# A decoder layer on one core: a first chunk's product one place later, a sum in another buffer, a split ahead of copies, and unit runs that end in half depths

## The chip, the cores and the metric

The kernel runs on one core of a Trainium2 chip. The metric is device time in microseconds (us) of one launch. The engines are called TensorE (PE; PEld is its weight load), VectorE (DVE), ScalarE (ACT), GpSimd (POOL) and SyncE (SP, which issues the transfers).

## The reference, cut to what matters

```
mod = silu(c) @ w_ada + b_ada                       # six rows: shift, scale, gate for two sub-layers
h = rms_norm(x, g_pre_mix) * (1 + sc_m) + sh_m      # x is 1024 tokens x 1024
proj = h @ w_in                                     # 256 pooling channels, then q, k, v: 12 heads of 64
q, k = partial_rope(q), partial_rope(k)
o_g = dilated_window_attention(q, k, v)             # three groups of 4 heads: dilation 1, 4, 16
attn = sum_g softmax_over_g(lse_g) * o_g
x = x + gt_m * rms_norm(concat(pool(u), attn) @ w_out, g_post_mix)
h = rms_norm(x, g_pre_ffn) * (1 + sc_f) + sh_f
gate, val = split(h @ w_up)                         # 2 x 2816 columns
y = (gelu(causal_conv3(gate)) * val) @ w_down
x = x + gt_f * rms_norm(y, g_post_ffn)
```

All is float32. The kernel multiplies float32 by splitting each factor in a high part and the rest (a copy on ScalarE that rounds, and a subtraction on VectorE, called the lower) and adding three products: high by high, high by low, low by high.

## The kernel before, in words

The attention stage handles six units, each one dilation group and one pair of heads, in the order (2,0), (1,0), (0,0), (2,1), (1,1), (0,1); a unit's number in the code is `ui`, from 0. `project(un, prev)` runs the unit's input product over eight token tiles `t`, each eight deep in `k` (`mm`, which calls `proj_mm`, three matmuls of 128x384, and then `Q.tick()`). So one unit has 64 ticks. The queue `Q` carries out the attention of the unit before, a piece at a time, on ticks: turning q and k (`turn_qk`, L621), scores (L680), turning the weights (L700), weighing values (L710) and turning the merged result (`turn_a`, L752). The tile's product lies in PSUM bank `t % 2`; `evac` copies q and k to SBUF on ScalarE (L265) and v on VectorE (L267, L270). Two tiles make a pair `m`, which is then rotated (`rope`). The unit's weights lie in four pieces of two `k` each (`ws[k // 2]`). The buffers for pieces number six; the next unit's pieces are asked for at ticks 2, 10, 50 and 56, so its third and fourth take the buffers of the current unit's first two (split: ScalarE L123, VectorE L170). In this stage only TensorE's order is the order of the text; the orders of the other engines are chosen when the program is compiled.

Behind it comes the channel sub-layer, in which the order of every engine but SyncE is the order of the text. Its first product, a chunk of 128 gate and 128 value columns at a time (22 chunks `c`), is computed by seven products of half size instead of eight (a Strassen-Winograd form). Four half-size sums of the activations (`sums`, on VectorE) and their splits (`parts`) are made once, in column halves `lo_t` and `hi_t`. A product `(n, c)` has twelve matmuls of 128x512. Products 1 and 2 of the first four chunks run ahead; then a list `steps` sets the order of the rest: places 0 to 3 are (5,0), (6,0), (3,0), (7,0), written out by hand, places 4 to 8 are (5,1), (6,1), (4,0), (3,1), (7,1), and place 9 is (5,2). Product 4 of chunk 0 needs the split of activation block "22", which is made only when chunk 0's others are on their way.

`prep(n, c)` makes a product's weights: for n of 5, 6, 7 and 4 a sum on GpSimd (`total`, L1158: t1, t2, t3, t4), then the high copy on ScalarE (L123); the lower (L1154) is returned and called a place or so later by `prep_up(to, low)`, which prepares up to place `to` and calls the lowers below `low`. Sums and fetched weights take their buffers in turn from `pool_r`; the pieces take theirs in turn from `ring`, of which `more0` lies in the memory of the activations that "22" is split from. The loaded weights of a chunk lie in `raw4`; t4 of chunk 0 is made in the buffer `b21`. `later_evac` puts the evictions of a product one place later (`at_step`): n of 6 frees the banks of 5 and 6, 3 and 7 and 4 their own; 4 is followed by the convolution's taps (L1189, L1191), a gelu on ScalarE and the gating product (L1196). PSUM has eight banks, taken in the order in which they came free.

Of the kernel before, what the change touches and what calls it, by code (L numbers as in the profile page):

```python
# [76 lines left out]
TURN_AT = ((5, 5, 0, 0), (6, 2, 0, 1), (6, 7, 1, 0), (7, 2, 1, 1), (8, 3, 2, 0), (8, 7, 2, 1), (9, 7, 3, 0), (10, 3, 3, 1))  # L77
# [27 lines left out]
def block_kernel(ctx: ExitStack, tc: tile.TileContext, x, pos, cols, rows, consts, w_ada_a, w_ada_b, w_in_u,  # L105
# [155 lines left out]
    def evac(un, t, b):  # L261
        m, j = divmod(t, 2)
        if m not in un.qs:
            un.qs[m] = bq.tile([P, 2, 256], F32, name="qs", tag="qs", bufs=2)
        nc.scalar.activation(un.qs[m][:, j], PS[:, b, 0:256], AF.Copy)  # L265
        if un.g == 0:
            nc.vector.tensor_copy(un.V[:, t], PS[:, b, 256:384])  # L267
            return
        vs = bq.tile([P, P], F32, name="vs", tag="vs", bufs=2)
        nc.vector.tensor_copy(vs, PS[:, b, 256:384])  # L270
        if un.g == 1:
            dst = vscr[1].rearrange("(r n i) c -> n i r c", r=4, n=2)[t // 4, 32 * (t % 4):32 * (t % 4) + 32]
        else:
            dst = vscr[2].rearrange("(r i) c -> i r c", r=16)[8 * t:8 * t + 8]
        nc.sync.dma_start(dst, vs)
# [14 lines left out]
    un = Unit(0, None)  # L290
# [308 lines left out]
    with tc.tile_pool(name="bp", bufs=1) as bp, tc.manual_schedule(engines={ET.PE}):  # L599
# [39 lines left out]
        def project(un, prev):  # L639
            def mm(t, lo=0, hi=NK):  # L640
                for k in range(lo, hi):
                    proj_mm(bank(t % 2, 384), t, un.ws, k)
                    Q.tick()

            def turned(m):
                Q.after(LAG_QK if un.ui else LAG_0, lambda: turn_qk(un, m), lambda: prev is None or prev.scored == NT)

            if un.ui == 0:
                turned(0)
                for m in (1, 2):  # L650
                    mm(m + 5, 0, 4)
                    for t in range(2 * m, 2 * m + 2):
                        evac(un, t, t)
                    rope(un, m)
                    turned(m)
            for m in range(0 if un.ui else 3, 4):
                for t in range(2 * m, 2 * m + 2):
                    mm(t, 0 if un.ui else 4)
                    evac(un, t, t % 2)
                rope(un, m)  # L660
                turned(m)
# [150 lines left out]
        for ui in range(5):  # L812
            if ui:
                un = Unit(ui, ws)
# [27 lines left out]
        un = Unit(5, ws)  # L842
# [34 lines left out]
    if True:  # L877
# [56 lines left out]
        def parts(name, cols, of=(0, 1), lo_eng=None):  # L934
            for k, h, l in A[name][of[0]:of[-1] + 1]:
                split(SRC[name][:, k:k + h.shape[1], cols], h[:, :, cols], l[:, :, cols], lo_eng=lo_eng)
# [10 lines left out]
        def sums(cols, which):  # L947
            m11, m12, m21, m22, m1 = (x[:, :, cols] for x in (a11, a12, a21, a22, SRC["s1"]))
            for i in which:
                o, a, b, op = ((m1, m22, m21, ALU.subtract), (m11, m1, m11, ALU.add), (m12, m11, m12, ALU.subtract),  # L950
                               (m21, m11, m22, ALU.subtract))[i]
                nc.vector.tensor_tensor(o, a, b, op)
# [25 lines left out]
        if True:  # L978
            def slot(key):
                if key in TURNS:  # L980
                    x_turn(*TURNS[key])
                    h_split(*TURNS[key])
# [11 lines left out]
            for c in range(AHEAD + 1):  # L994
                if c == 0:
                    up_load(2)
                    up_load(3)
                if c == 2:
                    raws = [rp.tile([P, 2, 512], F32, name="raws", tag="raw") for _ in range(2)]
                    raws = [t[:, i] for t in raws for i in range(2)]  # L1000
                    for i in range(4):
                        nc.sync.dma_start(raws[i], w_up[0, :, i])
                    b11, b21, b12, b22 = raws
                    t2r = cp.tile([P, 512], F32, name="t2r", tag="macc")
                    p0 = r2.tile([P, 4, 512], F32R, name="p0", tag="r2b")
                    ring += [(p0[:, i], p0[:, i + 1]) for i in (0, 2)]
                    TR["t4", 0] = b21
                for n in range(8):
                    slot((8 + c, n))
                    if (8 + c, n) == FIRST_T:  # L1010
                        start_sum("t1", b11, b11, b12)
                        start_sum("t2", t2r, b11, b22)
                        start_piece("t1", b11)
                        start_piece("t2", t2r)
                    if (8 + c, n) == TURN_AT[-2][:2]:
                        sums(lo_t, range(4))
                        parts("s1", lo_t)
                        parts("s2", lo_t)
                    if (8 + c, n) == LAST_X:
                        stats((), (NT - 1,))  # L1020
                        s1 = r2.tile([P, 2] + half[1:], F32R, name="s1", tag="r2c")
                        A["s1"] = [(0, s1[:, 0], s1[:, 1])]
                        SRC["s1"] = r2.tile(half, F32, name="s1t", tag="r2a")
                        pairs_of("s2")
                    wh, wl = (x[:, n * P:(n + 1) * P] for x in wu[c])
                    ah, al = side("11" if n < 4 else "12", n % 4)
                    o = bank(SLOTS[c][n // 4])
                    nc.tensor.matmul(o, wh, ah, start=n % 4 == 0, stop=False)
                    nc.tensor.matmul(o, wh, al, start=False, stop=False)
                    nc.tensor.matmul(o, wl, ah, start=False, stop=n % 4 == 3)  # L1030
# [25 lines left out]
            def first(c):  # L1056
                if c < NC_FF:
                    first_copy(c)
                    first_add(c)
# [73 lines left out]
            A["22"] = [(0, *(r2.tile(half, F32R, name="b22", tag=t) for t in ("r2a", "r2b")))]  # L1133
            s1g = cp.tile([P, 512], F32, name="s1g", tag="cst")
            gm = r1.tile(half, F32, name="gm", tag="rb1")
            pool_r = [b22, b11, b12, gm[:, 2], gm[:, 3], b21]

    gscr = tc.dram_tile([NC_FF // 2, 7, P, 512], F32, name="gscr")
    gtf_d = tc.dram_tile([1, D], F32, name="gtf_d")
    if True:  # L1140
# [70 lines left out]
        steps, done, START_AT = [], AHEAD, {}  # L1211
        for c in range(NC_FF):
            START_AT[c] = len(steps)
            one = []
            if c not in SKIP and done < NC_FF - 1:
                done += 1
                one = [done]
            ahead = [(n, k) for n in (2, 1) for k in one]
            old = [(4, c - 1)] * (c > 0)
            if c in SKIP or not ahead:  # L1220
                steps += [(5, c), (6, c)] + old + [(3, c), (7, c)]
            else:
                steps += [(5, c)] + old + [(6, c)] + ahead + [(3, c), (7, c)]
        steps.append((4, NC_FF - 1))
# [30 lines left out]
        def at_step(i, f, rank=0):  # L1255
            tasks.append((i, rank, len(tasks), f))
            tasks.sort(key=lambda t: t[:3])
# [21 lines left out]
            for kb in range(8):  # L1279
                EXTRA.setdefault(i - 18 + 2 * kb, []).append(lambda hf=hf, kb=kb: gate_acc(hf, kb))  # L1280
        for c in range(1, NC_FF - 1):
            EXTRA.setdefault(START_AT[c] + 5, []).append(lambda c=c: at_step(now[0], lambda: first(c + 1)))

        DOWN = (1, 2, 6, 5, 3, 7, 4)
        KD = NC_FF // 2
# [32 lines left out]
        def prep_up(to, low):  # L1318
            while ready[0] < min(to, len(steps)):
                lows.append(prep(*steps[ready[0]]))  # L1320
                ready[0] += 1
            while lows and ready[0] - len(lows) < min(low, len(steps)):
                lows.pop(0)()
# [4 lines left out]
        at["p"] = 0  # L1328
        prep_up(6, 6)
        evac(3, 0)  # L1330
        parts("22", all_t)
        evac(7, 0)
        for i, (n, c) in enumerate(steps):
            if i < 4:
                continue
            now[0] = i
            for f in EXTRA.get(i, ()):
                f()
            to = i + 1 + min(LEAD, 2 + (i - 4) // 3)
            prep_up(to, to - LAG_LO)  # L1340
            left = len(steps) - i
            if left <= 5:
                if not R1:
                    R = r1.tile([P, 16, 512], F32, name="R1", tag="ra")
                    R1 += [R[:, j] for j in range(KD)]
                    extend(pool_r, "r", [raw4[0][:, j] for j in range(4)] + [R[:, j] for j in range(KD, 16)])
                for j in {5: (0, 1), 4: (2,), 3: (3,), 1: (4,)}.get(left, ()):
                    prep_down(j)
            run_tasks(i)
            while not idle:  # L1350
                run_tasks(10**6, 1)
            product(n, c)
            later_evac(n, c)
            if (n, c) == (5, NC_FF - 1):
                more = r2.tile([P, 8, 512], F32R, name="tail", tag="r2c")
                extend(ring, "p", [(more[:, 2 * j], more[:, 2 * j + 1]) for j in range(4)])
# [147 lines left out]
```

## Time and profile before

| | |
|---|---|
| median of three runs | 1061.61 us (1061.49 to 1061.78) |
| the profiled execution, its own time | 1063.7 us |
| its span, first to last instruction | 1061.8 us |
| TensorE busy | 1033.1 us, 97% of the span |
| VectorE busy | 857.9 us, 81% |
| ScalarE busy | 486.8 us, 46% |
| GpSimd busy | 217.8 us, 21% |
| mean granted clock of TensorE | 0.996 |

The busy share is an average over stages. A matmul's end is modelled, so idle time of TensorE is better read from starts than from ends. A granted clock of 1.00 is 2.4 GHz, 0.50 would be 1.2 GHz, and a number between is a stretch that had both.

### The profile page before, as it was taken

Reading aid. Unit: us, or ns where it says so; the run is one execution under the profiler, and the core shown is the slowest. Engines: PE = TensorE matmul, PEld = TensorE weight load, DVE = VectorE, ACT = ScalarE, POOL = GpSimd, SP = SyncE. Lnnn points to the kernel's source line nnn. Section 1 sums busy time; section 2 is a strip of 40 time slices with the busy share of each in tenths; the row PEclk is TensorE's granted clock in tenths of the full one; section 3 lists DMA queues with packets and bytes.
Section 4 is the critical chain, followed back from the end, with each engine's and each line's share of the span. In section 5 each row is a group of like instructions: output and inputs, shape, how many; then the busy total and the mean of one; then the engine's idle time right before and its main releaser. Section 6 shows DMA issues by size and latency. Waiting matters only on the chain.

```text
span 1061.8 us, 15438 instructions
## 1 busy us (share of the span) xinstructions
PE 1033.1 (97%) x5174; PEld 875.2 (82%) x5174; DVE 857.9 (81%) x1839; ACT 486.8 (46%) x964; POOL 217.8 (21%) x132
## 2 busy tenths in 40 slices
PE   5999999999999999999999999999999999999997
PEld 4988989889888787878888888888888888888885
DVE  7974467876457768999999888999998898756998
ACT  6764343433354469643343333333333265544642
POOL 0000000000000000154433333244333415103560
PEclk9999999999999999999999999999999999999999
DMA  9552346352131173324335334444453879466563
GB/s 365 214 170 75 111 115 215 83 182 72 54 96 46 37 257 128 111 90 159 127 131 169 138 116 144 158 149 159 169 174 114 308 240 375 159 197 219 183 213 119
DMA packets 85148, 168.34 MB, mean 159 GB/s; under 512 B 9158, under 2 KB 25926, under 8 KB 81356
## 3 DMA queue, kind: packets, MB, share of 16 engines
q1 hardware_dynamic: 85068, 167.35, 46.8%
q8 instruction: 41, 0.67, 0.3%
q14 instruction: 39, 0.32, 0.1%
HBM read 134.47 MB, written 32.84 MB: 158 GB/s over the span
## 4 chain that ended last, share of the span: by engine, by line
PE 88%; DVE 5%; ACT 3%; DMA 2%; issue 2%; POOL 0%; SPq 0%; DVEq 0%; ACTq 0%; POOLq 0%
PE PS L1084 36%; PE PS L1384 20%; PE PS L221 6%; PE PS L223 5%; PE PS L222 5%; PE PS L710 3%; PE PS L680 2%; PE PS L700 1%; DVE acc L343 1%; PE PS L595 1%; PE PS L597 1%; PE PS L596 1%; DMA wa<-in_w_ada_a_dram 1%; PE PS L621 1%; PE PS L776 1%
## 5 line engine op out<-in xcount | busy, mean ns | idle before, releaser
L1158 POOL TENSOR_TENSOR raws<-rw 128x512 f32<-128x512 f32 x30 | 47.9, 1598 | 503.8 <-DVE raws L962 446.4
L221 PE MATMUL PS<-wh,hh 128*128 128x384 f32 x336 | 125.4, 373 | 1.3 <-DVE vs L270 1.2
L223 PE MATMUL PS<-wh,hl 128*128 128x384 f32 x336 | 113.8, 339 | 0.0
L222 PE MATMUL PS<-wl,hh 128*128 128x384 f32 x336 | 113.5, 338 | 0.0
L1084 PE MATMUL PS<-a,more 128*128 128x512 f32 x408 | 95.4, 389 | 0.0
L1384 PE MATMUL PS<-tail 128*128 128x512 f32 x384 | 91.4, 389 | 0.0
L123 ACT ACTIVATE more<-raws 128x512 fp32r<-128x512 f32 x79 | 49.4, 627 | 88.1 <-PE PS L1084 74.9
L1084 PEld LDWEIGHTS PS<-a,more 128*128 128x128 f32 x408 | 76.6, 188 | 15.9
L1384 PEld LDWEIGHTS PS<-tail 128*128 128x128 f32 x384 | 72.0, 188 | 15.0
L221 PEld LDWEIGHTS PS<-wh,hh 128*128 128x128 f32 x336 | 64.0, 190 | 9.7 <-issue 4.8
L1384 PE MATMUL PS<-more 128*128 128x512 f32 x300 | 70.1, 389 | 0.0
L1154 DVE TENSOR_TENSOR more<-raws,more 128x512 fp32r<-128x512 f32 x74 | 66.6, 903 | 2.1 <-PE PS L1084 2.1
L689 ACT ACTIVATE pm<-pm,nm 128x128 f32<-128x128 f32 (+1 forms) x96 | 42.4, 443 | 51.8 <-DVE nm L687 34.9
L1384 PEld LDWEIGHTS PS<-more 128*128 128x128 f32 x300 | 56.3, 188 | 11.7
L222 PEld LDWEIGHTS PS<-wl,hh 128*128 128x128 f32 x336 | 64.0, 190 | 0.6 <-issue 0.5
L683 DVE CUSTOM_DVE_ANT_0 pm<-PS,cst 128x128 f32<-128x128 f32 (+1 forms) x96 | 30.6, 348 | 41.5 <-PE PS L680 38.0
L1084 PE MATMUL PS<-b,more 128*128 128x512 f32 x252 | 61.9, 394 | 2.0 <-DVE more L1154 2.0
L223 PEld LDWEIGHTS PS<-wh,hl 128*128 128x128 f32 x336 | 63.5, 189 | 0.0
L1084 PE MATMUL PS<-s,more 128*128 128x512 f32 x252 | 61.8, 394 | 0.4 <-DVE more L1154 0.4
L1084 PEld LDWEIGHTS PS<-b,more 128*128 128x128 f32 x252 | 47.8, 190 | 12.3 <-DVE more L1154 2.4
L1084 PEld LDWEIGHTS PS<-s,more 128*128 128x128 f32 x252 | 47.2, 188 | 11.8 <-issue 1.3
L1193 ACT ACTIVATE cv<-cv 128x1024 f32<-128x1024 f32 x22 | 23.4, 1062 | 67.8 <-DVE cv L1191 67.8
(341 smaller groups left out, 2484.7 us busy)
## 6 DMA issues: line engine op xcount, KB each, us to landing
rw<-in_w_up_dram SPq DMA_DIRECT2D x21, 1024.0 KB
gscr<-VV SPq DMA_DIRECT2D x66, 256.0 KB
mraw<-in_w_ada_b_dram SPq DMA_DIRECT2D x48, 256.0 KB
R<-in_w_down_dram SPq DMA_DIRECT2D x48, 256.0 KB
raw<-in_w_in_u_dram SPq DMA_DIRECT2D x24, 384.0 KB
wa<-in_w_ada_a_dram SPq DMA_DIRECT2D x8, 1024.0 KB
R<-gscr SPq DMA_DIRECT2D x27, 256.0 KB
raws<-in_w_up_dram SPq DMA_DIRECT2D x25, 256.0 KB
```

The lines of the kernel that those rows point to most:

```text
L123: nc.scalar.activation(o, i, AF.Copy)
L221: nc.tensor.matmul(o, a, wh[:, c0:c0 + 384], start=k == 0, stop=False)
L222: nc.tensor.matmul(o, a, wl[:, c0:c0 + 384], start=False, stop=False)
L223: nc.tensor.matmul(o, b, wh[:, c0:c0 + 384], start=False, stop=k == 7)
L683: nc.vector.tensor_tensor_reduce(out=pm[:, h, 0:nk * P], in0=PS[:, 2 + h, 0:nk * P], in1=mask, op0=ALU.add, op1=ALU.max, scale=1.0, scalar ...
L689: nc.scalar.activation(pm[:, h, 0:nk * P], pm[:, h, 0:nk * P], AF.Exp, bias=nm[:, h:h + 1], scale=0.125, accum_out=U[:, h, HD + 1:HD + 2])
L710: nc.tensor.matmul(PS[:, 6, h * HD:(h + 1) * HD], pt[:, i * P:(i + 1) * P], un.V[:, k0 + kb, h * HD:(h + 1) * HD], start=kb == 0, stop=kb ...
L1084: nc.tensor.matmul(o, w_[:, k * P:(k + 1) * P], side(a, k)[low], start=i == 0, stop=i == 11)
L1154: nc.vector.tensor_tensor(wl, r, wh.bitcast(F32), ALU.subtract)
L1158: nc.gpsimd.tensor_tensor(t, a, b, ALU.add)
L1193: nc.scalar.activation(cv, cv, AF.Gelu_apprx_tanh)
L1384: nc.tensor.matmul(o, g[:, ts_], w, start=k == 0 and j == 0, stop=k == KD - 1 and j == 2)
```

## The change

Four places of the text change. In unit runs 1 to 5 the first half of the depth of token tiles 6 and 7 is computed for both before the second half of either. In the list of places, chunk 1 has (3,1) ahead of (4,0); with it the preparation of these two is spread around the split of "22" and the evictions of (7,0), and `first(c + 1)` gets a rank that puts it behind the other tasks of its place. The list of sum buffers has `b21` second instead of last. The sums of the columns `lo_t` and the split of the first of them stand ahead of the turn and copies of place (9, 7) instead of behind.

```
@@ project
             for m in range(0 if un.ui else 3, 4):
+                if un.ui and m == 3:
+                    mm(6, 0, 4)
+                    mm(7, 0, 4)
                 for t in range(2 * m, 2 * m + 2):
-                    mm(t, 0 if un.ui else 4)
+                    mm(t, 0 if un.ui and m < 3 else 4)
@@ first products of the channel sub-layer
+                    if (8 + c, n) == TURN_AT[-2][:2]:
+                        sums(lo_t, range(4))
+                        parts("s1", lo_t)
                     slot((8 + c, n))
...
                     if (8 + c, n) == TURN_AT[-2][:2]:
-                        sums(lo_t, range(4))
-                        parts("s1", lo_t)
                         parts("s2", lo_t)
@@ buffers
-            pool_r = [b22, b11, b12, gm[:, 2], gm[:, 3], b21]
+            pool_r = [b22, b21, b11, b12, gm[:, 2], gm[:, 3]]
@@ places
-                steps += [(5, c), (6, c)] + old + [(3, c), (7, c)]
+                steps += [(5, c), (6, c)] + ([(3, c)] + old if c == 1 else old + [(3, c)]) + [(7, c)]
@@ tasks
-            EXTRA.setdefault(START_AT[c] + 5, []).append(lambda c=c: at_step(now[0], lambda: first(c + 1)))
+            EXTRA.setdefault(START_AT[c] + 5, []).append(lambda c=c: at_step(now[0], lambda: first(c + 1), 1))
@@ ahead of the places
         prep_up(6, 6)
         evac(3, 0)
+        prep_up(7, 7)
         parts("22", all_t)
+        prep_up(8, 7)
         evac(7, 0)
+        prep_up(8, 8)
```

## Rows read from the trace of the kernel before

**Rows 1.** The chain that ended last: start, length, what
```profile
461.84 251.25 PE PS L1084 x1100
```
**Rows 2.** TensorE's waits: us in total, times, longest
```profile
PE PS L1084 <- DVE more L1154: 2.4, 2, 2.0
```
**Rows 3.** Windows, 220 to 232 us: busy and count by engine, PEclk, DMA
```profile
220.00:224.00 4.00, 1.91 (x12) 1.59 (x11) 3.94 (x15) 2.11 (x5) 0.00 (x0) 0.96 0.62 197
224.00:228.00 4.00, 4.00 (x16) 3.97 (x16) 2.71 (x15) 1.73 (x4) 0.00 (x0) 0.61 0.50 168
228.00:232.00 4.00, 4.00 (x27) 3.96 (x26) 4.00 (x8) 1.28 (x3) 0.00 (x0) 1.00 0.58 174
```
**Rows 4.** Timeline of TensorE in unit 3: start, length, [idle before]
```profile
223.81 0.48 PE L752 MATMUL PS<-cst,at 128*128 128x128 f32 x1 [2.09 <-ACT kT L123]
...
227.57 0.27 PE L752 MATMUL PS<-cst,at 128*128 128x128 f32 x1
```
**Rows 5.** Timeline of VectorE in unit 3
```profile
217.49 0.29 DVE L125 COPY U<-PS 128x128 f32<-128x128 f32 x1 [0.39 <-PE PS L710]
...
220.09 0.28 DVE L270 COPY vs<-PS 128x128 f32<-128x128 f32 x1
...
221.59 0.96 DVE L170 TENSOR_TENSOR wl<-raw,wh 128x768 fp32r<-128x768 f32 x1
...
222.53 0.58 DVE L125 COPY qT<-PS 128x256 f32<-128x256 f32 x1
...
225.55 0.47 DVE L746 SCALAR_TENSOR_TENSOR at<-U,sm,at 128x64 f32<-128x64 f32 x2
```
**Rows 6.** Timeline of ScalarE in unit 3
```profile
219.55 0.85 ACT L123 ACTIVATE wh<-raw 128x768 fp32r<-128x768 f32 x1 [1.10 <-PE PS L223]
...
223.15 0.61 ACT L123 ACTIVATE kT<-PS 128x256 f32<-128x256 f32 x1 [1.59 <-DVE dn L739]
```
**Rows 7.** Timeline of TensorE, places 6 to 12
```profile
458.79 1.07 PE L1084 MATMUL PS<-b,more 128*128 128x512 f32 x4
461.84 3.14 PE L1084 MATMUL PS<-b,more 128*128 128x512 f32 x8 [1.98 <-DVE more L1154]
464.78 1.68 PE L1084 MATMUL PS<-s4h,more 128*128 128x512 f32 x4
...
468.14 1.07 PE L1084 MATMUL PS<-s3h,more 128*128 128x512 f32 x4
...
479.02 1.30 PE L1084 MATMUL PS<-a,p 128*128 128x512 f32 x5
```
**Rows 8.** Timeline of VectorE, 434 to 477 us
```profile
434.70 0.69 DVE L170 TENSOR_TENSOR p<-raws,p 128x512 fp32r<-128x512 f32 x1
...
457.20 2.79 DVE L170 TENSOR_TENSOR b<-raw_a,b 128x2048 fp32r<-128x2048 f32 x1
...
461.11 0.68 DVE L1154 TENSOR_TENSOR more<-raws,more 128x512 fp32r<-128x512 f32 x1
...
471.15 1.28 DVE L1191 SCALAR_TENSOR_TENSOR cv<-GG,col,cv 128x1022 f32<-128x1022 f32 x1
...
476.08 0.67 DVE L1098 TENSOR_TENSOR VV<-VV,PS 128x512 f32<-128x512 f32 x1
```
**Rows 9.** Timeline of GpSimd, 453 to 461 us
```profile
453.14 1.29 POOL L1158 TENSOR_TENSOR t2r<-raws,rw 128x512 f32<-128x512 f32 x1 [3.56 <-DVE raws L962]
454.39 1.74 POOL L1158 TENSOR_TENSOR raws<-rw 128x512 f32<-128x512 f32 x1
...
457.81 3.32 POOL L1158 TENSOR_TENSOR gm<-rw 128x512 f32<-128x512 f32 x1
```
**Rows 10.** Timeline of ScalarE, 431 to 468 us
```profile
431.86 1.93 ACT L925 ACTIVATE raw_a<-PS,bcol,acol 128x256 f32<-128x256 f32 x4
...
460.02 0.63 ACT L123 ACTIVATE more<-rw 128x512 fp32r<-128x512 f32 x1 [2.60 <-DVE b L170]
...
466.63 1.24 ACT L1102 ACTIVATE cv<-GG,col 128x1024 f32<-128x1024 f32 x1 [4.33 <-DVE GG L1101]
```

## The prediction

> **What bounds the kernel now.** I read the chain that ended last first. From 461.84 us on it is TensorE alone for 251 us [rows 1], and what follows to the end is almost all TensorE too, so a microsecond won or lost ahead of 461.84 reaches the end, unless another engine then falls behind. Next come TensorE's waits. The largest on VectorE's lowers is 2.4 us in two [rows 2], the larger of them 2.0 long, and one other wait of the same size, 2.09 us, stands in unit 3 of the attention stage [rows 4]. These two are what the change can reach. Each costs more than it shows. In the windows the granted clock is 0.96 in the 4 us of the wait and 0.61 in the next 4, so TensorE ran partly at its 1.2 GHz level after it; those 4 us hold 16 matmuls where the next hold 27 [rows 3]. Eleven matmuls at 4/27 us are about 1.5 us. For the second wait, take the starts of places 6 to 12 [rows 7]: places 8 to 11 take 479.02 - 468.14 = 10.88 us, 2.72 for a product, 0.227 for a matmul. Places 6 and 7 take 468.14 - 458.79 = 9.35 where 5.44 would do: 3.9 us lost, 2.1 of it idle (four matmuls from 458.79 end at 459.70, the fifth starts at 461.84), the other 1.8 slow matmuls (eight from 461.84 to 464.78 are 2.9 us in place of 1.8, place 7 is 3.36 in place of 2.72).
>
> The cause of both is VectorE's queue. In unit 3 the two lowers of the next unit's third and fourth pieces (0.96 each, one shown) stand ahead of the copy qT at 222.53; kT can follow only at 223.15, and the turn at 223.81 needs that bank [rows 4 to 6]. At place 6 the lower that product (4,0) waits for is at 461.11, behind the 2.79 us lower of "22" and two evictions of (7,0) [rows 8].
>
> **The change part by part.**
>
> *Half depths.* No matmul is added. In a unit's last sixteen products of one `k`, pieces 0 and 1 now have their last use four products sooner; the high copy, at 219.55 now and released by TensorE [rows 6], can start that much earlier. VectorE is nearly full there (3.94 of 4 us, [rows 3]), so an earlier start helps only as far as it fills idle time or lets something else go behind. Up to qT I find 0.39 us of idle that an earlier lower can fill, and the v copy of tile 6 (0.28, at 220.09) now falls due later than qT [rows 5]: 0.67 us. That leaves 1.4 us of the 2.09. If the compiled order also puts qT ahead of the second lower, 0.96 more goes, and 0.5 stays. With a shorter wait the slow matmuls (1.5) should go, since no other wait of 1.4 us or less shows a fallen clock in this trace; that is my choice, the other end being that they stay. So the first turn comes 2.2 us earlier. What is late next is the second turn, at 227.57: the merged result that it turns is ready at 225.55 + 0.47 = 226.0 [rows 4, 5], a margin of 1.55; with the same 0.67 us from VectorE it can start 2.2 us earlier at most. Both give 2.2. Bounds: 0 (VectorE does the same in the same order), and 2.1 + 1.5 = 3.6. I take 2.2. The other units show no such wait, so I cost them at nothing: their cover is that tile 6's eviction still has four products of tile 7 after it.
>
> *First sum and split ahead of the copies.* ScalarE's copy of the split no longer stands behind the four copies of the turn, which wait for TensorE, so VectorE's lower needn't wait. But the next split on ScalarE stands behind the other four copies in either kernel, which end at 431.86 + 1.93 = 433.8 [rows 10]. Its copy (0.63) then ends at 434.4 and the lower that now starts at 434.70 [rows 8] starts some 0.3 us earlier. All that follows on VectorE up to place 4 goes with it: 0.3 us, bounds 0 and 0.5.
>
> *Places 6 and 7 and their preparation.* (3,1) now takes a free piece and needs neither "22" nor `more0`. Its copy and lower stand ahead of the split of "22". (4,0) now takes `more0`, so its copy waits for the lower of "22", as (3,1)'s does in the row at 460.02 [rows 10]. VectorE: lower (3,1) 0.6; lower of "22" 2.4 (at the 0.6 for 512 columns of the small ones; 2.79 with a sum beside it), from 457.2 to 459.6; two evictions to 460.8; lower (4,0) to 461.45. TensorE, 0.3 us earlier, starts (3,1) at 458.5 and ends it at 461.2; (4,0) needs its lower after four matmuls, at 462.1. No wait, and both end at 463.9 in place of 468.14: **4.2 us**.
>
> *The buffer.* With `b21` second, the sum t3 of chunk 1 is written where (4,0)'s weights are read from, so it waits for lower (4,0), and every GpSimd sum behind it waits too. Before, t3 ran at 454.39 and the third sum behind it was done by 461.1 [rows 9]; now t3 starts at 461.5. This is also what frees the lowers before 461 of the sums beside them. How the two engines meet is in the rows: the lower of "22" ends at 460.0, and the sum at 457.81 beside it ends 1.14 after that, 3.32 long in place of 1.29 [rows 8, 9]. So they take turns. The Trainium skill (SBUF — State Buffer, Who interferes with whom) states that VectorE and GpSimd contend for a shared port pair through an exclusive lock; the trace agrees (3.32 against 1.29 us). By this rule the postponed sums can't hide beside lowers, which speaks against the change and for the 2.6 us worked out next rather than 4.2.
>
> Taking turns from 461.45, with 1.3 for a sum and 0.63 for a copy: sum t3 to 462.8, copy 463.45, lower (7,1) behind the second sum 464.65; third sum (t1 for (5,2)) 465.8, copy 466.45, lower (5,2) behind the fourth sum 467.65; eviction of (3,1) 468.25, lower (4,1) 469.35, eviction of (4,0) 469.95, lower (6,2) 471.05. Then `cv` on ScalarE (1.24) ends at 471.2, two taps with one or two sums between (1.2 each and 1.1 a sum) bring VectorE to 474.7 or 475.8, and two evictions of (7,1) to 475.9 or 477.0. TensorE: (7,1) from 463.9 (copy 463.45), (5,2) from 466.65 (copy 466.45), (4,1), (6,2), and place 12, (2,4), at 474.8. It takes the bank of (7,1), so it waits until 475.9 to 477.0. Before, it started at 479.02, with that bank free since 476.75 [rows 7, 8]. Of 4.2 + 0.3 us **2.0 to 3.1 stay; I take 2.6** (0.3 for the split included). The bounds are 1.0 (the wait at place 12 lets the clock fall) and 4.5. Later places have more room than place 12 had.
>
> The rank of `first` changes no order that I can find; the other tasks of its place already stand ahead. Nothing.
>
> **Sum.** 2.2 + 2.6 = 4.8 us. The profiled execution would go from 1063.7 to 1058.9, its span from 1061.8 to 1057.0. The median of the runs is 1061.61, 0.2 below the span; I predict **1056.8**, by itself 1055.3 to 1058.4.
>
> **The rivals.**
>
> *Nearly all is kept.* VectorE finds its place 12 eviction early, because sums and lowers seldom meet, and the compiled order puts qT ahead. For it: VectorE gets to the end of lower (4,0) 2 us sooner than it now gets to the end of both lowers. Against: the row at 457.81. 4.5 + 2.7 = 7.2 us: 1054.4. Chance 0.15.
>
> *Unit 3's wait only moves.* The first turn is earlier, the second waits as long, since VectorE has no time to give (3.94 of 4 us). Only 2.6 us: 1059.0. Chance 0.20.
>
> *The postponed sums take back the channel part.* If three sums last 2.7 us each (between the 1.74 and 3.32 of the rows) t1 for (5,2) lands at 469.6 and its copy at 470.2. TensorE waits 3.5 us from 466.65, starts (5,2) 0.6 before its time now, and pays some 1.7 in slow matmuls. So -1.1 there, +2.2 in unit 3: 1060.5. Chance 0.14.
>
> *Slower: tile 6's bank.* A unit's tile 6 now ends four products (some 2.1 us, 0.53 each with no attention between) before the next unit wants its bank, instead of eight. In unit 3 its v copy ended at 220.37, about 2.3 us after the product, behind other VectorE work [rows 5]. If the compiled order puts the two lowers and a copy ahead of it in all five units, the bank is 3.5 us late, 1.4 us of wait each, 7 in all: 1061.6 + 7.0 - 4.8 = 1063.8. It decides from about 3.5 us of delay; at 2.3 it costs 1 us. Chance 0.06.
>
> **How the numbers follow.** My forecast has 0.45. 0.2%, 2.1 us, is about what a measurement of this kernel can tell from no change: below 1059.5 is faster, above 1063.7 slower. Faster: the forecast, the first rival and three quarters of the second, 0.74. Slower: 0.07 (the fourth and a little of the unknown). Same: 0.19. The range, 1054.2 to 1060.4, reaches from the first rival's time to just short of the third's; it leaves out the fourth (0.06), half of the third (0.07) and a little below (0.05).
>
> **What would show it.** In the profile after: the wait of 2.09 us at L752 in unit 3 down to 1.4 or less, with the granted clock at 1.00 behind it; places 6 and 7 without a wait on a lower, 5.4 us for both; t3 on GpSimd starting right behind lower (4,0), near 459 (461.5 less unit 3's gain); a new wait of TensorE on an eviction of (7,1) at place 12, 1 to 2 us. No wait there means the first rival; a wait of TensorE on the copy for (5,2) the third; waits on v copies at unit starts the fourth. The prediction is wrong if the orders compiled for ScalarE and VectorE in the attention stage change elsewhere, which no row of the kernel before can show.

## The result, and the profile after

The changed kernel took 1063.36 us, the median of 22 runs (1061.19 to 1065.09); the kernel before, beside it, 1061.76 (22 runs, 1060.10 to 1063.52). The ratio is 1.0015 (1.0008 to 1.0021). The forecast was 1056.8, its range 1054.2 to 1060.4. The profiled execution took 1064.49 with a span of 1062.7, against 1063.7 and 1061.8; TensorE is still 97% busy in it, VectorE 80%. Lines of the changed kernel stand three to seven further on: L1158 is the lower, L1088 the product, L1095 and L1096 evict products 6 and 5, L1101 and L1102 evict product 7, L1193 and L1195 are the taps.

TensorE's waits in the kernel after (columns as in [rows 2]):

```profile
PE PS L1088 <- DVE UU L1095: 2.3, 1, 2.3
PE PS L1088 <- DVE VV L1102: 1.8, 1, 1.8
...
PE PS L755 <- DVE at L749: 1.5, 1, 1.5
...
PE PS L1088 <- DVE more L1158: 0.4, 1, 0.4
```

The 2.0 us on a lower [rows 2] are gone. In their place stand two waits on evictions, 4.0 us together. Where they are, TensorE's timeline of the kernel after shows, from unit 3 to place 24:

```profile
222.01 0.30 PE L755 MATMUL PS<-cst,at 128*128 128x128 f32 x1 [0.25 <-DVE sm L736]
...
225.88 0.33 PE L755 MATMUL PS<-cst,at 128*128 128x128 f32 x1 [1.48 <-DVE at L749]
...
456.40 1.07 PE L1088 MATMUL PS<-s4h,more 128*128 128x512 f32 x4
...
459.12 2.88 PE L1088 MATMUL PS<-b,more 128*128 128x512 f32 x12
461.84 1.07 PE L1088 MATMUL PS<-s3h,more 128*128 128x512 f32 x4
...
474.66 2.98 PE L1088 MATMUL PS<-a,p 128*128 128x512 f32 x12 [1.78 <-DVE VV L1102]
...
507.16 4.56 PE L1088 MATMUL PS<-s,more 128*128 128x512 f32 x12 [2.26 <-DVE UU L1095]
511.52 1.15 PE L1088 MATMUL PS<-s2h,more 128*128 128x512 f32 x4
```

Up to place 12 it went nearly as forecast, in this pair of executions. Unit 3's first turn waits 0.25 in place of 2.09 us [rows 4]; places 6 and 7 take 5.44 us (456.40 to 461.84) in place of 9.35 [rows 7]; place 12 starts at 474.66, 4.36 us ahead of 479.02 [rows 7]. Then place 23, product (5,4), waits 2.26 us, and its twelve matmuls take 4.36 (507.16 to 511.52) in place of 2.72: 1.64 of slow matmuls. Of the 4.36 us 0.14 are left when place 24 starts (511.52, before 511.66). The first matmul of the gate rows, further on, starts at 712.90 us, before at 712.93.

Most of the 4.36 us is not the change's. The profiled execution of the kernel before had slow matmuls in unit 3 and at place 6 [rows 3, 7]. From the first matmul of unit 1 to place 12 it takes 407.58 us (71.44 to 479.02), the kernel after 402.93 (71.73 to 474.66), and the kernel before with another order behind place 7 ("Evictions ahead in the kernel before", below), whose clock stayed at 1.00 in both stretches, 404.10 (71.58 to 475.68). So the change itself is 1.2 us ahead at place 12, behind its wait there, and 3.5 us are slow matmuls.

The cause is in VectorE's timeline of the kernel after:

```profile
455.07 2.29 DVE L170 TENSOR_TENSOR b<-raw_a,b 128x2048 fp32r<-128x2048 f32 x1 [0.44 <-ACT b L123]
...
458.47 0.69 DVE L1158 TENSOR_TENSOR more<-raws,more 128x512 fp32r<-128x512 f32 x1
...
461.23 1.11 DVE L1158 TENSOR_TENSOR more<-raws,more 128x512 fp32r<-128x512 f32 x1 [0.75 <-ACT more L123]
464.20 1.23 DVE L1158 TENSOR_TENSOR more<-raws,more 128x512 fp32r<-128x512 f32 x1 [1.86 <-ACT more L123]
...
469.07 2.02 DVE L1193 SCALAR_TENSOR_TENSOR cv<-GG,col,cv 128x1023 f32<-128x1023 f32 x1 [0.22 <-ACT cv L1106]
471.12 2.20 DVE L1195 SCALAR_TENSOR_TENSOR cv<-GG,col,cv 128x1022 f32<-128x1022 f32 x1
473.24 0.67 DVE L1101 TENSOR_TENSOR UU<-UU,PS 128x512 f32<-128x512 f32 x1
...
501.95 2.25 DVE L1193 SCALAR_TENSOR_TENSOR cv<-GG,col,cv 128x1023 f32<-128x1023 f32 x1 [0.71 <-ACT cv L1106]
504.23 2.18 DVE L1195 SCALAR_TENSOR_TENSOR cv<-GG,col,cv 128x1022 f32<-128x1022 f32 x1
506.34 0.67 DVE L1095 TENSOR_TENSOR UU<-UU,PS 128x512 f32<-128x512 f32 x1
```

It ends the lower of "22" 2.6 us sooner than before (457.36 against 459.99, [rows 8]), and then idles 0.75 and 1.86 us on copies of sums that GpSimd has only just made. The first of these sums, in GpSimd's timeline of the kernel after, stands right behind the lower of (4,0); before, it ran at 454.39 [rows 9]:

```profile
459.24 1.29 POOL L1162 TENSOR_TENSOR raws<-rw 128x512 f32<-128x512 f32 x1 [7.20 <-DVE more L1158]
```

Ahead of both evictions that TensorE waits for stand two taps of 2.0 to 2.25 us each. The eviction for place 23 starts at 506.34. In the kernel before, VectorE's and TensorE's timelines have it a microsecond sooner, with TensorE 2.9 us later than its end:

```profile
505.35 0.68 DVE L1091 TENSOR_TENSOR UU<-UU,PS 128x512 f32<-128x512 f32 x1
```

```profile
508.94 2.88 PE L1084 MATMUL PS<-s,more 128*128 128x512 f32 x12
```

So TensorE came earlier and VectorE did not. In the chain that ended last, the stretch of TensorE alone that began at 461.84 [rows 1] begins at place 23 now:

```profile
507.16 205.91 PE PS L1088 x900
```

Another 0.90 us of the profiled execution went after 845 us: from the first matmul of the down projection to the last it takes 210.13 us, before 209.23. The twelve traces of the experiments have 209.21 to 209.27, also with all parts of the change in them, so no part of it is shown to cause this; it is left open.

### The profile page after: what moved, and what is told of

It reads as the page before. It is cut to its first block, busy times and chain, and to the rows that moved or that the text cites. A ratio compares the mean times of both kernels' runs of the same rounds, so it can differ in the third digit from the quotient of the medians.

```text
span 1062.7 us, 15439 instructions
## 1 busy us (share of the span) xinstructions
PE 1031.1 (97%) x5174; PEld 872.2 (82%) x5174; DVE 855.2 (80%) x1839; ACT 488.3 (46%) x964; POOL 212.7 (20%) x132
## 4 chain that ended last, share of the span: by engine, by line
PE 79%; DVE 12%; ACT 3%; DMA 3%; issue 2%; POOL 0%; SPq 0%; DVEq 0%; ACTq 0%
PE PS L1088 32%; PE PS L1391 15%; PE PS L221 6%; PE PS L223 5%; PE PS L222 5%; PE PS L713 3%; PE PS L683 2%; PE PS L703 1%; DVE acc L343 1%; PE PS L595 1%; PE PS L597 1%; PE PS L596 1%; DVE more L1158 1%; DMA wa<-in_w_ada_a_dram 1%; PE PS L621 1%
## 5 line engine op out<-in xcount | busy, mean ns | idle before, releaser
L1088 PE MATMUL PS<-a,more 128*128 128x512 f32 x408 | 95.4, 389 | 0.0
L1088 PEld LDWEIGHTS PS<-a,more 128*128 128x128 f32 x408 | 76.6, 188 | 15.9
L1158 DVE TENSOR_TENSOR more<-raws,more 128x512 fp32r<-128x512 f32 x74 | 67.8, 920 | 5.3 <-PE PS L1088 2.7
L1088 PE MATMUL PS<-s,more 128*128 128x512 f32 x252 | 63.5, 401 | 2.7 <-DVE UU L1095 2.3
L1088 PE MATMUL PS<-b,more 128*128 128x512 f32 x252 | 60.5, 389 | 0.0
L1088 PEld LDWEIGHTS PS<-s,more 128*128 128x128 f32 x252 | 48.0, 191 | 14.8 <-issue 4.0
L1088 PEld LDWEIGHTS PS<-b,more 128*128 128x128 f32 x252 | 47.3, 188 | 9.8
```

The costliest lines, as they stand in the source:

```text
L1088: nc.tensor.matmul(o, w_[:, k * P:(k + 1) * P], side(a, k)[low], start=i == 0, stop=i == 11)
L1158: nc.vector.tensor_tensor(wl, r, wh.bitcast(F32), ALU.subtract)
```

## The experiments

Two theories. One: the order of VectorE's queue gives the gain back, the taps ahead of the evictions. Two: VectorE has too much to do up to place 23 in any order, so what is won ahead of it can't arrive. The kernel before took 1062.06 to 1062.08 us beside each of the three sets of runs.

### Parts of the change

**Half depths alone**, on the kernel before:

```
+                if un.ui and m == 3:
+                    mm(6, 0, 4)
+                    mm(7, 0, 4)
-                    mm(t, 0 if un.ui else 4)
+                    mm(t, 0 if un.ui and m < 3 else 4)
```

> The kernel before with the half depths alone. Theory 1 (from place 5 to place 23 of the channel part VectorE sets the pace; what TensorE wins ahead of it stays only if VectorE wins it too): VectorE reaches the channel part 1.7 us earlier as well, the wait of 2.1 us at place 6 and its slow matmuls stay, nothing else waits, and the 1.7 us arrive at the end: about 1060. Theory 2 (VectorE gets to places 12 to 23 at the same time whatever stands ahead, so nothing won ahead of it arrives): no change.

1060.78 us (1059.97 to 1062.62), ratio 0.9989 (0.9979 to 0.9998). The second turn of unit 3 waits 1.5, place 6 still 2.0. A small gain by itself; what it is made of shows further down.

**The change with the old order of the sum buffers:**

```
-            pool_r = [b22, b21, b11, b12, gm[:, 2], gm[:, 3]]
+            pool_r = [b22, b11, b12, gm[:, 2], gm[:, 3], b21]
```

> The changed kernel with the sum buffers in their old order, so that chunk 1's t3 needn't wait for the lower of (4,0). Theory 1: VectorE's two idle stretches for copies of sums (0.75 and 1.86 us in the changed kernel, between places 7 and 8) go, VectorE reaches place 12's eviction some 2 us earlier, TensorE's waits at place 12 (1.8) and place 23 (2.3, with 1.7 of slow matmuls behind it) shrink to 0.5 or less each: 3 to 4 us faster than the changed kernel, about 2 faster than before. Rival (the sums then meet the lowers ahead of 461 us again and cost there what they save later): lower (4,0) is late by 1 to 2 us, and the time is that of the kernel before within 1 us.

1060.74 us (1060.12 to 1061.20), ratio 0.9987 (0.9978 to 0.9996): 2.6 under the change. Place 7 waits 1.36 and 0.50 us, place 12 not at all, place 23 0.48. The postponed sums save 1.86 us and cost 1.78 and 1.78.

**The change without half depths** (the first diff taken out):

> The changed kernel without the half depths. Theory 2 (place 23's eviction comes at a time that VectorE sets by itself): TensorE's wait at place 23 is shorter by the 1.7 us that the half depths gave, perhaps short enough to leave the clock alone, and the time is that of the changed kernel or up to 1.5 us better. Theory 1: VectorE starts the channel part 1.7 us later, is later at place 23 by as much, and the kernel is 1.7 us slower than the changed one.

1063.33 us (1061.82 to 1064.03), the change's own time. The waits at places 12 and 23 are 1.77 and 2.37.

**The new buffer order alone**, on the kernel before (the second diff's lines the other way round):

> The kernel before with the new order of the sum buffers alone. Places 6 and 7 keep their old order, so t3 of chunk 1 waits for the lower of (4,0) at 461.11 us minus what the absent sums save. Theory 1: the wait of 1.98 us at place 6 shrinks to 0.5 to 1.5 (no sum beside the lower of the second block), and TensorE waits at place 12 and 23 on evictions behind taps instead: 1061.5 to 1063.5. If the postponed sums were harmless by themselves: 1059.5 to 1060.5, with no wait at place 23.

1061.69 us (1061.30 to 1063.43), ratio 0.9997 (0.9988 to 1.0006). The wait at place 6 shrinks to 1.17 and one of 1.54 appears at place 12, none at place 23. The wait is split in two, not removed.

### The order of VectorE's queue

**Taps behind everything else of their place:**

```
-            at_step(i + 1, lambda: taps(c, g))
+            at_step(i + 1, lambda: taps(c, g), 2)
```

> The changed kernel with the two taps of a chunk ranked behind the other tasks of their place, so that evictions that free banks stand ahead of them. Theory 1: the evictions of (7,1) and (6,3) are 4 us earlier, the waits at places 12 and 23 are gone with the slow matmuls, nothing else of VectorE's work changes: 4 to 5 us faster than the changed kernel, 2.5 to 4 faster than before. Rival (the taps' later end makes the gelu, the gating product and what reads them late, and the waits only move): within 1 us of the changed kernel.

1057.95 us (1057.48 to 1058.58), ratio 0.9961 (0.9949 to 0.9974), no wait at places 12 and 23. Here first's add also stands ahead of the taps and overwrites half of the gate chunk that they read, so they compute something else; the instructions and their number are the same. With the same work in another order the time falls by 5.4 us: theory two can't hold for the whole.

**Evictions ahead of the taps, first behind them:**

```
-            at_step(i + 1, lambda: taps(c, g))
+            at_step(i + 1, lambda: taps(c, g), 1)
...
-            ... at_step(now[0], lambda: first(c + 1), 1)
+            ... at_step(now[0], lambda: first(c + 1), 2)
```

> The kernel after, with the taps of a chunk ranked behind the evictions of their place (and first's add behind the taps); nothing else differs. Theory 1 (the gain of places 6 and 7 is lost where VectorE has two taps of about 2 us each ahead of the eviction that frees TensorE's bank): the waits of 1.78 us at place 12 and 2.26 us at place 23 go, with the slow matmuls behind the second; the gate product, at 712.90 us in the profile after, comes 4.5 to 5.5 us sooner; time about 1058, and at most 1059. Theory 2 (VectorE has too much to do between places 6 and 23 in any order, so what is won ahead of it can't arrive): the evictions come sooner but other VectorE work later, new waits of 1.5 us or more on lowers or evictions stand at places 13 to 26, and the time is 1061.5 to 1063.5.

1059.95 us (1059.23 to 1061.73), ratio 0.9981 (0.9973 to 0.9990). That is between the two theories' numbers. Place 23 waits no more, but in place 12 TensorE waits in its last third, on the lower p; TensorE's, VectorE's and ScalarE's timelines of this kernel:

```profile
476.27 1.21 PE L1088 MATMUL PS<-a,p 128*128 128x512 f32 x4 [1.78 <-DVE p L1158]
```

```profile
471.06 2.19 DVE L1195 SCALAR_TENSOR_TENSOR cv<-GG,col,cv 128x1022 f32<-128x1022 f32 x1
474.93 0.69 DVE L1058 TENSOR_TENSOR GG<-UU,PS 128x512 f32<-128x512 f32 x1 [1.67 <-ACT UU L123]
475.53 0.69 DVE L1158 TENSOR_TENSOR p<-gm,p 128x512 fp32r<-128x512 f32 x1
```

```profile
473.35 1.06 ACT L1197 ACTIVATE cv<-cv 128x1024 f32<-128x1024 f32 x1 [4.02 <-DVE cv L1195]
474.31 0.58 ACT L123 ACTIVATE UU<-PS 128x512 f32<-128x512 f32 x1
```

The lower stands behind first's add, which waits for first's copy on ScalarE, which stands behind the gelu, which waits for the taps. So VectorE idles 1.67 us ahead of a lower that TensorE waits for.

**The same with the old buffer order:**

> The same with the old order of the sum buffers: the sums of GpSimd are not postponed, but meet the lowers of places 6 and 7. With the old order and taps ahead of evictions (1060.7) TensorE waited 1.36 and 0.50 us at place 7 and 0.48 us at place 23. Theory 1: the 0.48 goes and the waits of place 7 stay, so 1060 to 1060.6, 2 us more than with b21 second: what the buffer is worth once the evictions are not behind the taps. Theory 2: the buffers alone were the harm, so this is the best of the four, at 1058.5 or less.

1060.48 us (1059.81 to 1062.40), ratio 0.9986 (0.9978 to 0.9995): the waits of place 7 (1.36 and 0.51) stay and the 0.48 goes, as expected; the gap to the kernel above is smaller than expected because of that one's wait at place 12. The new order of the buffers had been 2.6 us the worse; now the medians are 0.5 us apart the other way, and their intervals overlap, so the two orders are no longer told apart.

**Evictions ahead, first's copy too, its add behind the taps:**

```
+            def split_first(c):
+                at_step(now[0], lambda: first_copy(c + 1), 0.5)
+                at_step(now[0], lambda: first_add(c + 1), 2)
-            ... at_step(now[0], lambda: first(c + 1), 2)
+            ... split_first(c)
```

> The kernel with evictions ahead of the taps, and first's copy of the bank (UU, ScalarE) ahead of the taps too, so that it stands ahead of the gelu; first's add stays behind the taps. Theory 1 (the 1.78 us that TensorE waits at place 12 in that kernel is now on the lower p, because first's add stands ahead of it and waits 1.67 us for a copy behind the gelu): the idle 1.67 us of VectorE and TensorE's wait go, no wait over 0.5 us stands between places 6 and 30, the gate product comes near 706.8 in place of 708.55, the time is 1057.8 to 1058.6. Theory 2 (VectorE's work limits these places in any order): the 1.78 us come back at place 23 or another, and the time stays at 1059.5 to 1060.5.

**1058.27 us** (1057.78 to 1059.49), ratio 0.9965 (0.9953 to 0.9977): faster than both kernels, at their full computation. TensorE's timeline, places 12 and 23, and VectorE's behind the taps:

```profile
475.02 1.19 PE L1088 MATMUL PS<-a,p 128*128 128x512 f32 x4 [0.24 <-DVE p L1158]
...
503.26 2.88 PE L1088 MATMUL PS<-s,more 128*128 128x512 f32 x12
```

```profile
471.37 2.20 DVE L1195 SCALAR_TENSOR_TENSOR cv<-GG,col,cv 128x1022 f32<-128x1022 f32 x1
473.67 0.69 DVE L1058 TENSOR_TENSOR GG<-UU,PS 128x512 f32<-128x512 f32 x1
474.28 0.68 DVE L1158 TENSOR_TENSOR p<-gm,p 128x512 fp32r<-128x512 f32 x1
```

The first gate matmul starts at 707.26 us in place of 712.90. Theory two falls: with the buffers of the change, the same work in another order brings the gain to the end of the kernel. The postponed sums are the other half of the cause, since with the old buffers the taps ahead of the evictions cost only the 0.48 us at place 23.

**Evictions ahead in the kernel before** (the ranks 1 and 2 of the first such kernel, nothing else):

> The kernel before with evictions ahead of the taps alone. Theory 1 (before, places 12 and 23 had room, since TensorE came late to them after its wait at place 6): the wait of 1.98 us at place 6 stays, nothing is won, 1061.5 to 1062.5, and the gate product stays within 0.3 us of 712.9 less what slow matmuls cost there. If the order were worth something by itself: 1060.5 or less.

1061.95 us (1060.15 to 1063.82), ratio 0.9997 (0.9987 to 1.0007). Nothing, as theory one has it: TensorE, held 1.99 us at place 6, comes late enough for the evictions.

### The half depths and the split, with nothing behind that takes a gain back

**Evictions ahead, no half depths**, and **the best kernel without half depths:**

> The evictions ahead of the taps, without the half depths. Theory 1 (nothing behind takes a gain back any more): unit 3's wait of about 2.1 us at the first turn returns in place of about 1.5 at the second, with or without slow matmuls behind it, and the time is 0.5 to 2.2 us over that with the half depths. If the half depths are worth nothing even then, it is within 0.3 us of it.

> The same without the half depths, with nothing left behind that could take a gain back. If the half depths only move unit 3's wait from the first turn to the second (2.1 us there against 0.25 and 1.5): unit 3 costs 0.3 to 0.4 us more in idle time, and 1.5 more in an execution whose matmuls are slow behind the wait; the median is 0.3 to 2 us over that with the half depths. If they are worth the 2.2 us of the prediction in every execution: 2 us or more over.

The first took 1060.87 us (1059.43 to 1061.22), against 1059.95 with half depths; the second 1058.01 (1057.69 to 1059.82), against 1058.27. The second pair's medians don't tell them apart. In its traces the first gate matmul is at 707.57 without and at 707.26 with, 0.31 us; but 0.29 of that stands already at the first matmul of unit 1 (71.83 and 71.54), ahead of every half depth. What differs between the two kernels without half depths is the matmuls behind unit 3's wait. That wait is 2.09 to 2.10 us in every kernel without half depths; the window 224 to 228 us behind it, for the first of these kernels and then the second (columns as in [rows 3]):

```profile
224.00:228.00 4.00, 4.00 (x16) 3.91 (x15) 3.42 (x14) 1.84 (x5) 0.00 (x0) 0.57 0.56 173
```

```profile
224.00:228.00 4.00, 4.00 (x24) 3.97 (x25) 3.60 (x17) 2.51 (x5) 0.00 (x0) 1.00 0.62 199
```

The one fell to a granted clock of 0.57, with 16 matmuls; the other kept 1.00, with 24.

**The best kernel with the split behind the copies again:**

```
-                    if (8 + c, n) == TURN_AT[-2][:2]:
-                        sums(lo_t, range(4))
-                        parts("s1", lo_t)
                     slot((8 + c, n))
...
+                        sums(lo_t, range(4))
+                        parts("s1", lo_t)
                         parts("s2", lo_t)
```

> The same kernel (with half depths) but with the first sum and its split back behind the turn and copies of their place. If the move is worth the 0.3 us that the prediction gave it: the gate product comes 0.2 to 0.5 us later, the time 0.3 us more, which is only to be seen in the trace. If it is worth nothing: the starts of places 4 and on agree within 0.1 us once unit 3 is taken off.

1058.97 us (1058.46 to 1060.60), 0.70 more. Place 0 starts 0.28 us later (439.42 against 439.14), place 6 0.98 (457.47 against 456.49): 0.70 lies between them, over the 0.2 to 0.5 expected. The other traces agree: from place 0 to place 6 it is 18.00 to 18.05 us in the five with the split behind the copies, 17.34 to 17.39 in the nine with it ahead. The first lower of the split, in VectorE's timeline without the move and then with it:

```profile
429.60 1.23 DVE L170 TENSOR_TENSOR s<-s1t,s 128x1024 fp32r<-128x1024 f32 x1 [0.80 <-ACT s L123]
```

```profile
428.44 1.22 DVE L170 TENSOR_TENSOR s<-s1t,s 128x1024 fp32r<-128x1024 f32 x1
```

## Why the prediction was wrong

**The step that failed** is "Later places have more room than place 12 had", which put the cost of all later places at nothing. In the trace that I read it was true: at place 23 TensorE came 508.94 - 506.03 = 2.9 us after the eviction it needed, at place 12 479.02 - 476.75 = 2.3. But TensorE was to come 4.8 us sooner by the sum, more than either, and a margin only holds if the other engine comes sooner by the difference. And part of that room was made by the slow matmuls of that one execution. With half depths alone, whose clock stayed at 1.00 in unit 3 and behind place 6, VectorE's and TensorE's timelines at places 12 and 23 show 1.4 us (476.04 - 474.67) and 1.2 (505.96 - 504.72):

```profile
474.00 0.67 DVE L1101 TENSOR_TENSOR VV<-VV,PS 128x512 f32<-128x512 f32 x1
...
504.04 0.68 DVE L1094 TENSOR_TENSOR UU<-UU,PS 128x512 f32<-128x512 f32 x1
```

```profile
476.04 2.88 PE L1087 MATMUL PS<-a,p 128*128 128x512 f32 x12
...
505.96 2.88 PE L1087 MATMUL PS<-s,more 128*128 128x512 f32 x12
```

I followed VectorE's queue to place 12 and no further. Its lead was spent there. From the second eviction of (6,1) to the end of chunk 0's taps it takes 13.45 us in the kernel after (459.79 to 473.24), and 8.23 for the same work with half depths alone (462.72 to 470.95): 2.8 more are idle, for the most part on postponed sums, 1.6 more are in lowers and 0.7 in taps that ran beside these sums. Counted from the first matmul of unit 1, VectorE comes to the eviction for place 23 2.5 us later than with half depths alone (506.34 - 71.73 against 504.04 - 71.95). So what the runs showed in place of more room is a VectorE that the postponed sums make late, and two taps ahead of the eviction: 2.26 us of wait at place 23.

**Places 6 and 7** went as worked out: (3,1) and (4,0) without a wait in 5.44 us, the lower of "22" at 2.29 for 2.4, t3 right behind the lower of (4,0). But the 9.35 us that I set against it held slow matmuls: the kernel before with evictions ahead, at a clock of 1.00, takes 7.74 (457.06 to 464.80), so 2.3 us are won there and not 3.9.

**Place 12** too: a wait of 1.78 on the eviction of (7,1), forecast 1 to 2. The third rival's wait, on the copy for (5,2), didn't come; its mechanism, postponed sums that make VectorE late, did, at a place that I hadn't looked at.

**The half depths** were sized at 2.2 us and give 0.1 or less where the clock holds. From the first matmul of unit 1 to place 0 it is 367.44 us with half depths alone (71.95 to 439.39) and 367.48 in the kernel before with evictions ahead (71.58 to 439.06); 367.33 in the kernel after and 367.44 without its half depths. The second rival was right here: the first turn is earlier and the second waits 1.48, since its merged result is made by the same full VectorE. The margin of 1.55 that I read at the second turn was made by the slow matmuls ahead of it, which I let go in the same sum. In the change without half depths, where the clock was 1.00, VectorE's and TensorE's timelines show the merged result ready at 225.84 and the second turn 0.18 us behind it:

```profile
225.36 0.48 DVE L746 SCALAR_TENSOR_TENSOR at<-U,sm,at 128x64 f32<-128x64 f32 x2
```

```profile
226.02 0.27 PE L752 MATMUL PS<-cst,at 128*128 128x128 f32 x1
```

The other part of the 2.2, slow matmuls of 1.5 us (eleven at 4/27 are 1.6), is there in some executions only. The record has each run's mean granted clock. Of the 27 runs of the kernel before beside half depths alone, 7 have 0.999 and took 1060.05 to 1060.64 us; the other 20 have 0.994 to 0.998 and took 1061.57 to 1064.18. With half depths 8 of 11 have 0.999 (1059.97 to 1061.31), and 3 have 0.997 (1062.01 to 1062.62). So at the same clock the two kernels take the same time, and the 1.28 us of the medians are a fallen clock in fewer runs.

**The split** was sized at 0.3 with bounds of 0 and 0.5, and measures 0.7. I let its lower wait behind the next copy; it is the first lower that gains, its 0.80 us of idle, and with it goes a wait of 0.21 us at product (7,0).

**The rank of first** I gave no effect. With chunk 0's product one place later, its taps share place 9 with first(2), whose add overwrites what they read, so the rank keeps first behind them. And its copy behind the gelu is what cost 1.78 us once the evictions were ahead.

**The sum, without slow matmuls,** read from starts, against the kernel before with evictions ahead: 0.1 (half depths) + 0.66 (split: place 0 to 6) + 2.30 (places 6 and 7) - 2.04 (places 8 to 12, 15.64 for 13.60) - 2.47 (places 13 to 23, 34.03 less 1.64 of slow matmuls for 29.92) = -1.45 us, so the change costs about a microsecond and a half. The shortest run of each, 1060.10 before and 1061.19 after, differ by 1.09, the medians by 1.60. Slow matmuls weigh on both kernels, on before in unit 3 and at place 6, on after at place 23; that the two medians are moved by about as much is not shown.

## What to carry to other kernels

When one engine is moved ahead, follow the other's queue to every later place where the two meet, and compare the lead with the smallest margin there, not with the margin where the gain is made. In a queue that runs in order, put the eviction that frees a bank, and the copy that a later add needs, ahead of long work that nobody is waiting for. An edit that loses (a sum postponed) is worth testing again once the order behind it is mended: here it no longer lost. And price a wait without the slow matmuls behind it, unless several executions show that they come each time.

## What the runs showed of the hardware

**A wait of the same length lowers the clock in one execution and not in the next.** Behind place 23's wait the window 507 to 511 us, in the kernel after (a wait of 2.26 us) and in the one without half depths (2.37):

```profile
507.00:511.00 4.00, 3.84 (x11) 3.11 (x12) 3.97 (x7) 3.74 (x7) 0.55 (x1) 0.65 0.28 90
```

```profile
507.00:511.00 4.00, 3.67 (x16) 3.06 (x17) 3.96 (x7) 3.83 (x7) 0.72 (x1) 1.00 0.30 97
```

The longer wait kept 1.00, which is 2.4 GHz; the shorter one had 0.65, partly 1.2 GHz. The kernel before, one and the same, has a mean clock of 0.999 in 7 of the 27 runs above and of 0.994 to 0.998 in the others. I had counted the slow matmuls of [rows 3, 7] as part of each wait; they are a chance beside it.

**What a sum on GpSimd slows on VectorE.** A tap takes 1.27 to 1.30 us alone and up to 2.35 beside sums. A lower of 512 columns, which reads SBUF twice, takes 0.68 or 0.69 alone, 1.1 to 1.2 beside them and 1.79 at the longest. But the 152 evictions of this stage in the kernel after, of the same size with one operand in PSUM, all take 0.67 to 0.69. One of them stands in the middle of a sum that ends at 468.29, in VectorE's and GpSimd's timelines of the kernel after:

```profile
467.07 0.68 DVE L1105 TENSOR_TENSOR GG<-UU,PS 128x512 f32<-128x512 f32 x1
```

```profile
466.56 1.73 POOL L1162 TENSOR_TENSOR raws<-t2r,rw 128x512 f32<-128x512 f32 x1
```

The Trainium skill (SBUF — State Buffer, Who interferes with whom) has the exclusive lock between these two engines for a VectorE instruction with two SBUF inputs beside a GpSimd one that reads SBUF, and no contention for one with at most one SBUF input. The lowers and taps agree with the first, and the evictions with the second.
